# A hybrid decoder layer on one core: side work tied to its stage, down products in column pairs, the last product closed half by half

## The chip, the cores and the metric

The kernel runs on one core of a Trainium2 chip. The metric is the device time of one execution in microseconds. Before the change three runs gave 2251.72 us as the median, from 2249.6 to 2251.99 us. A core has TensorE (PE, with its weight loads shown as PEld), VectorE (DVE), ScalarE (ACT), GpSimd (POOL) and SyncE (SP), which here issues nearly all transfers. Each engine works through its own list of instructions in order; what one needs from another it waits for.

## The reference

One layer over 2048 tokens of width 1024, all in float32:

```
mod = silu(c) @ w_ada + b_ada                     # six rows of 1024: shift, scale, gate, twice
h = rmsnorm(x) * (1 + scale1) + shift1
q, k, v, z, xbc, dt = split(h @ w_in)             # 2312 columns
attn = sliding_window_attention(rope(q), rope(k), v, sinks)      # window 128
y = gated_norm(ssd_chunked_scan(silu(conv(xbc)), dt), z)
x = x + gate1 * (concat(attn, y) @ w_out)
h = rmsnorm(x) * (1 + scale2) + shift2
x = x + gate2 * ((silu(h @ w_gate) * (h @ w_up)) @ w_down)       # width 2816
return rmsnorm(x) * final_w
```

## The kernel before, in words

The tokens are worked in four blocks of 512. Every float32 product is made of three products of rounded parts: each operand is split into a high part (written by ACT) and a low part (raw minus high, by DVE), and PE adds high*high, high*low and low*high into one PSUM bank (`mm3`, L274). So every weight and every activation costs an ACT and a DVE instruction before PE can use it.

The stages in order: an opening with the norm of block 0 and its modulation; the input projections of blocks 0 to 3 (`queries`, `keys_values`, `convolved`, `gated`), beside which attention and the SSD scan of earlier blocks are stepped ("sides"), and the output projections of blocks 0 and 1; then gate and up products of the first half of the tokens (`quads(0, ...)`), the output projections of blocks 2 and 3 (`first_output`, `second_output`), three down stages of the first half (`down0.stage`), gate and up of the second half (`quads(1, ...)`), and eleven more down stages. Gate/up and down use Strassen-like products: seven products of halves each, named b11, b21, t4, t2, t3, t1, b22; the down ones need sums of `w_down` blocks, made by `weight_sums` (L1048) and stored to `wd_s1` to `wd_s4`.

A loop that runs over main work calls `tick` after each step; a tick counts down `pending` entries, takes one step of the remaining modulation rows (`rest_of_ada`) and steps the sides by a ratio. This gives the order in which the code is traced. PE keeps it up to the end of the input projections (`manual_schedule`); DVE, ACT, POOL and SP are ordered by a scheduler that places an instruction as soon as its own estimate says that it can run, so an instruction without early inputs can stand far ahead of the code that traced it. `tc.issue_after(i)` keeps what is traced inside it behind instruction `i`.

Names to follow: `aw` are halves of `w_ada` rows (L192 loads, L197 reduces them on DVE with the row `csil`); `t` is a ring of eight 128x512 buffers (`tmp`); `hl` are the split activations of a block; `a` are split activations of the down stages; `ws` the blocks in `weight_sums`; `d`, `am`, `at`, `sm`, `st` are PSUM banks (four `d`, one of each other). `mid` is the residual in DRAM. In `steps_of` (L1075) a down stage has four output columns c, each with eleven k in three chunks, one weight tile per chunk.

Of the kernel before, what the change touches and what calls it, by code (L numbers as in the profile page):

```python
# [12 lines left out]
F32 = mybir.dt.float32  # L13
# [5 lines left out]
P = 128  # L19
# [25 lines left out]
def hymba_layer(ctx, tc, xT, xtok, pos, wada, wadk, vecs, rows, wq, wkv, wz, wx, wo, wgu, wd, outT):  # L45
# [140 lines left out]

    def ada_later(i):
        halves = [slice(0, T), slice(T, D)]
        ws = [big("aw", 2, pool=ip) for _ in halves]
        with tc.issue_after(mm3.last.ins):  # L190
            for w, hs in zip(ws, halves):
                nc.sync.dma_start(w, wada[i, :, hs])  # L192
# [3 lines left out]
        for w, hs, src, dst in zip(ws, halves, (b_ada[:, i:i + 1], pt), (pt, m)):  # L196
            nc.vector.tensor_tensor_reduce(w, w, csil[:, hs], 0.5, src, ALU.mult, ALU.add, dst)  # L197
# [126 lines left out]
    def modulated(x, bc, scale, shift, into):  # L324
        h = tmp()
        nc.vector.scalar_tensor_tensor(h, x, scale, bc, ALU.mult, ALU.mult)
        hi, lo = into
        nc.scalar.activation(hi, h, AF.Identity, bias=shift)
        modulated.last = nc.vector.scalar_tensor_tensor(lo, h, shift, hi.bitcast(F32), ALU.add, ALU.subtract)  # L329
        return hi, lo  # L330
# [16 lines left out]
    def norm1(b, h):  # L347
# [13 lines left out]
        yield  # L361
        for d in range(KT):
            h.append(modulated(load_x(b, d), bc, scl1[:, d:d + 1], sh1[:, d:d + 1], operand()))
        yield
# [190 lines left out]
    def attentions(b, m):  # L555
# [26 lines left out]
        held, nxt = None, load(0)  # L582
        for t in range(NT):
# [281 lines left out]
    def scaled(s, k, bc, which):  # L865

        h = {}
        for i, j in which:
            d = k + 4 * i
            x = h[i, j] = tmp()  # L870
            scaled.last = nc.sync.dma_start(x, mid[2 * s + j][d])
# [16 lines left out]
    def operands_first(s, ops, bc):  # L888

        for k in range(4):  # L890
            h = scaled(s, k, bc, ((0, 0), (1, 0)))
# [156 lines left out]
    def weight_sums(pool):  # L1048

        n = KP * P // 4  # L1050
        for c in range(4):
            for q in range(4):
                cs = slice(q * n, (q + 1) * n)
                a11, a21, a22, a12 = (small([P, n], "ws", 4, pool=pool) for _ in range(4))
                for x, (i, h) in ((a11, (0, 0)), (a21, (1, 0)), (a22, (1, 1)), (a12, (0, 1))):
                    nc.sync.dma_start(x, wd[c + 4 * i, h][:, cs])
                nc.vector.tensor_tensor(a11, a11, a21, ALU.subtract)
                nc.vector.tensor_tensor(a21, a21, a22, ALU.add)
                nc.vector.tensor_tensor(a22, a22, a11, ALU.subtract)
                nc.vector.tensor_tensor(a12, a12, a22, ALU.subtract)  # L1060
# [14 lines left out]
    def steps_of(act, src, banks, new, done, ts=slice(0, T), kept_w=None):  # L1075

        for c in range(4):
            if new:
                banks[c] = dense()
            ps = banks[c][:, ts]  # L1080
            for lo, hi in CHUNKS:
                key = c, lo
                if kept_w is not None and key in kept_w:
                    w = kept_w[key]
                else:
                    n = (hi - lo) * P
                    raw = wt.tile([P, 528], F32, name="raw", tag="raw", bufs=RAW)[:, 0:n]
                    nc.sync.dma_start(raw, src(c)[:, lo * P:hi * P])
                    if kept_w is None:
                        two = wt.tile([P, 2, 528], F32R, name="w", tag="w", bufs=SPLIT)  # L1090
                        w = two[:, 0, 0:n], two[:, 1, 0:n]
                    else:
                        a, b = pair("a", KP + 1, pool=steps_of.spare)
                        w = kept_w[key] = a[:, 0:n], b[:, 0:n]
                    nc.scalar.activation(w[0], raw, AF.Copy)  # L1095
                    nc.vector.tensor_tensor(w[1], raw, w[0].bitcast(F32), ALU.subtract)  # L1096
                for k in range(lo, hi):
                    ws = slice((k - lo) * P, (k - lo + 1) * P)
# [3 lines left out]
                if hi == KP:  # L1102
                    done(c, ps)
# [574 lines left out]
```

## Time and profile before

| what | value |
|---|---|
| median of three runs | 2251.72 us |
| the profiled execution's own time | 2250.91 us |
| its span | 2249.2 us |
| PE busy | 2172.1 us, 97% of the span |
| DVE busy | 1676.9 us, 75% |
| ACT, POOL busy | 1009.8 us, 573.6 us |
| transfers | 469.93 MB, mean 209 GB/s |

The profiled execution's time is 1.7 us above its span, and 0.8 us below the median. PE is the engine to read: what it does not work, or works at the lower clock, is the time that can be had; DVE is what it mostly waits for.

### The profile page before, as it was taken

The numbers are of one execution on the slowest core, as the hardware profiler recorded it, in microseconds if no ns is written. First come the engines' busy times: TensorE is split into PE (matmuls) and PEld (weight loads), VectorE is DVE, ScalarE is ACT, GpSimd is POOL, SyncE is SP. The second block draws the span as 40 slices with busy tenths as digits, with TensorE's granted clock in tenths as the row PEclk, the third lists the DMA queues.
The fourth block names the chain that finished last, engine by engine and source line by source line (L and its number), as shares of the span: only waits on it lengthen the run. The fifth ranks groups of instructions, "written<-read, shape, count | busy, mean of one in ns | idle before, by whom it ended". The sixth has DMA issues, their size and how long they took to land. (4 is left out here: it accounts for less than half of the span.)

```text
span 2249.2 us, 33574 instructions
## 1 busy us (share of the span) xinstructions
PE 2172.1 (97%) x11108; PEld 1806.9 (80%) x11108; DVE 1676.9 (75%) x3219; ACT 1009.8 (45%) x2135; POOL 573.6 (26%) x715
## 2 busy tenths in 40 slices
PE   8988999899999999999999999998999999999997
PEld 6877898789878788888888877786888888788887
DVE  8988876676569877788887667988767775786565
ACT  4564634554545654433344444532333333554342
POOL 0122433233112311144442311222323331220021
PEclk9999999999999999999999999999999999999999
DMA  8999988785879522333435678967323326777553
GB/s 288 333 396 310 325 264 302 235 285 186 294 267 309 168 85 93 101 119 106 127 103 164 222 251 281 348 210 233 116 94 113 99 90 206 260 265 266 173 171 101
DMA packets 289181, 469.93 MB, mean 209 GB/s; under 512 B 27376, under 2 KB 97008, under 8 KB 289008
## 3 DMA queue, kind: packets, MB, share of 16 engines
q1 hardware_dynamic: 288432, 467.27, 62.4%
q8 instruction: 87, 1.43, 0.3%
q14 instruction: 86, 0.70, 0.1%
q10 hardware_dynamic: 576, 0.52, 0.1%
HBM read 334.98 MB, written 132.71 MB: 208 GB/s over the span
## 5 line engine op out<-in xcount | busy, mean ns | idle before, releaser
L1100 PE MATMUL d<-a,w 128*128 128x512 f32 x1716 | 404.7, 396 | 5.6 <-DVE a L1072 2.6
L1100 PEld LDWEIGHTS d<-a,w 128*128 128x128 f32 x1716 | 321.5, 188 | 85.8 <-DVE a L1072 4.5
L961 PE MATMUL d<-b,w 128*128 128x512 f32 x924 | 367.8, 401 | 4.3 <-ACT t L985 3.4
L962 PE MATMUL d<-b,w 128*128 128x512 f32 x924 | 367.1, 397 | 3.0 <-DVE b L883 2.2
L963 PE MATMUL d<-b,w 128*128 128x512 f32 x924 | 366.6, 398 | 1.9 <-DVE w L853 1.9
L852 ACT ACTIVATE w<-s 128x512 fp32r<-128x512 f32 x176 | 110.7, 631 | 231.1 <-PE d L963 177.5
L961 PEld LDWEIGHTS d<-b,w 128*128 128x128 f32 x924 | 174.3, 189 | 45.0 <-ACT t L985 4.3
L962 PEld LDWEIGHTS d<-b,w 128*128 128x128 f32 x924 | 175.0, 189 | 42.8 <-DVE b L883 2.9
L963 PEld LDWEIGHTS d<-b,w 128*128 128x128 f32 x924 | 174.3, 189 | 42.0 <-DVE w L853 2.4
L275 PE MATMUL d<-w,hl 128*128 128x256 f32 (+1 forms) x592 | 174.7, 295 | 11.3 <-DVE so L504 3.1
L277 PE MATMUL d<-w,hl 128*128 128x256 f32 (+1 forms) x592 | 169.9, 287 | 3.2 <-DVE hl L329 2.9
L276 PE MATMUL d<-w,hl 128*128 128x256 f32 (+1 forms) x592 | 169.7, 287 | 0.8 <-DVE w L1310 0.8
L1096 DVE TENSOR_TENSOR w<-raw,w 128x512 fp32r<-128x512 f32 x156 | 105.8, 685 | 60.0 <-ACT w L1095 59.7
L853 DVE TENSOR_TENSOR w<-s,w 128x512 fp32r<-128x512 f32 x176 | 141.6, 806 | 9.7 <-ACT w L852 8.6
L285 POOL TENSOR_TENSOR acc<-acc,t 128x512 f32<-128x512 f32 x35 | 60.0, 1715 | 347.5 <-ACT t L284 338.3
L1095 ACT ACTIVATE w<-raw 128x512 fp32r<-128x512 f32 x156 | 91.1, 589 | 121.2 <-PE d L1100 83.5
L275 PE MATMUL d<-hl,w 128*128 128x512 f32 x352 | 144.8, 411 | 0.4 <-DVE s L385 0.4
L277 PE MATMUL d<-hl,w 128*128 128x512 f32 x352 | 139.3, 396 | 0.0
L276 PE MATMUL d<-hl,w 128*128 128x512 f32 x352 | 138.9, 395 | 0.2 <-DVE hl L812 0.2
L852 ACT ACTIVATE w<-raw 128x512 fp32r<-128x512 f32 x132 | 82.8, 630 | 115.2 <-PE d L963 45.6
L1072 DVE TENSOR_TENSOR a<-a 128x512 fp32r<-128x512 f32 x154 | 103.0, 694 | 36.8 <-ACT a L1071 36.5
L275 PEld LDWEIGHTS d<-w,hl 128*128 128x128 f32 x592 | 114.6, 194 | 15.5 <-DVE so L504 3.8
(420 smaller groups left out, 4919.7 us busy)
## 6 DMA issues: line engine op xcount, KB each, us to landing
raw<-in_wgu_dram SPq DMA_DIRECT2D x176, 256.0 KB, 2.8
w<-w_x SPq DMA_DIRECT2D x48, 512.0 KB, 5.3
act_t<-t SPq DMA_DIRECT2D x88, 256.0 KB, 3.2
a<-act_t SPq DMA_DIRECT2D x88, 256.0 KB, 4.7
act_b<-t SPq DMA_DIRECT2D x66, 256.0 KB, 2.1
a<-act_b SPq DMA_DIRECT2D x66, 256.0 KB, 4.8
aw<-in_wada_dram SPq DMA_DIRECT2D x64, 256.0 KB, 4.8
raw<-wd_s SPq DMA_DIRECT2D x64, 256.0 KB, 2.7
```

The costliest lines, as they stand in the source:

```text
L275: nc.tensor.matmul(out, ahi, bhi, start=first, stop=False)
L276: nc.tensor.matmul(out, ahi, blo, start=False, stop=False)
L277: mm3.last = nc.tensor.matmul(out, alo, bhi, start=False, stop=last)
L852: nc.scalar.activation(hi, x, AF.Copy)
L853: eng.tensor_tensor(lo, x, hi.bitcast(F32), ALU.subtract)
L961: nc.tensor.matmul(out, ahi, bhi, start=first and k == 0, stop=False, skip_group_check=True)
L962: nc.tensor.matmul(out, ahi, blo, start=False, stop=False, skip_group_check=True)
L963: mm3.last = nc.tensor.matmul(out, alo, bhi, start=False, stop=k == 3, skip_group_check=True)
L1072: nc.vector.tensor_tensor(lo, raw, hi.bitcast(F32), ALU.subtract)
L1095: nc.scalar.activation(w[0], raw, AF.Copy)
L1096: nc.vector.tensor_tensor(w[1], raw, w[0].bitcast(F32), ALU.subtract)
L1100: mm3.last = nc.tensor.matmul(ps, w[x][:, ws], act[k][y][:, ts], start=new and k == 0 and x + y == 0, stop=k == KP - 1 and x == 1, skip_gr ...
```

## The change: what it does

It has eight parts, with the lines of the new kernel in the order below.

1. **Modulation rows.** A helper `behind(engine)` gives an `issue_after` on the last instruction traced on that engine. The `aw` loads stand behind the last traced SP instruction, the reduces behind the last traced DVE instruction.
2. **Norm.** `modulated` works in place instead of through a second `t` buffer; `norm1` takes a block's eight columns in two halves, each half's loads one step ahead of its work. The tick numbers in `norm_ahead` change to match.
3. **Attention.** `attentions` yields once after its first load, and that step is taken at tick 10 of `convolved(0)`.
4. **Second norm's operands.** `operands_first` loads `mid` for step k+1 before it works on step k, and its DVE products stand behind the last traced DVE instruction.
5. **Output projection of block 3** uses the four `d` banks in place of `am` and `at` in turn.
6. **Weight sums.** Loads behind SP, sums behind DVE, with a step between them; 32 steps in place of 16, at twice the rate in `quads(1, ...)`.
7. **Down stages.** `steps_of` goes over columns in pairs: chunk 0 of both, chunk 1 of both, chunk 2 of both. The ratio of the side work beside the first three stages is 0.3 in place of 0.5, and the next stage's first eight `a` tiles are asked for at steps 8 and 9.
8. **Last product.** Still two halves of 256 tokens, but PE's order is now the code's, the squares' sums of half 0 are added on PE inside the next column, and half 0's root, spread and eight outputs are stepped inside half 1.

```diff
+    def behind(engine):
+        traced = nc.cur_bb.bb.instructions
+        return tc.issue_after(next(i for i in reversed(traced) if i.engine == engine))
...
-        with tc.issue_after(mm3.last.ins):
+        with behind(mybir.EngineType.SP):
             for w, hs in zip(ws, halves):
                 nc.sync.dma_start(w, wada[i, :, hs])
...
+        with behind(mybir.EngineType.DVE):
+            for w, hs, src, dst in zip(ws, halves, (b_ada[:, i:i + 1], pt), (pt, m)):
+                nc.vector.tensor_tensor_reduce(w, w, csil[:, hs], 0.5, src, ALU.mult, ALU.add, dst)
...
+        for ds in (range(KT // 2), range(KT // 2, KT)):
+            xs = [load_x(b, d) for d in ds]
+            yield
+            for d, x in zip(ds, xs):
+                h.append(modulated(x, bc, scl1[:, d:d + 1], sh1[:, d:d + 1], operand()))
+            yield
...
         held, nxt = None, load(0)
+        yield
...
+        x = fetched_mid(s, 0, which)
+        yield
         for k in range(4):
-            h = scaled(s, k, bc, ((0, 0), (1, 0)))
+            nxt = fetched_mid(s, k + 1, which) if k < 3 else None
+            with behind(mybir.EngineType.DVE):
+                h = scaled(s, k, bc, which, x)
+            x = nxt
...
+                with behind(mybir.EngineType.SP):
+                    for x, (i, h) in ((a11, (0, 0)), (a21, (1, 0)), (a22, (1, 1)), (a12, (0, 1))):
+                        nc.sync.dma_start(x, wd[c + 4 * i, h][:, cs])
+                yield
+                with behind(mybir.EngineType.DVE):
+                    nc.vector.tensor_tensor(a11, a11, a21, ALU.subtract)
...
-        for c in range(4):
-            if new:
+        for c, (lo, hi) in ((c + e, chunk) for c in (0, 2) for chunk in CHUNKS for e in range(2)):
+            if new and lo == 0:
                 banks[c] = dense()
...
+                        if at == 1:
+                            while late:
+                                late.pop(0)()
+                        step = part * (3 * c + at)
+                        for _ in range((step == 2 or step > 3) + (step == 6)):
+                            next(ends[0], None)
+                        yield
+                    done(part, c, ps)
...
-        yield from output(3)
+        yield from output(3, lambda c: dense())
...
-            if i >= 14 and i % 7 == 0:
+            if i >= 14 and i % 7 in (0, 4):
                 next(sums_of, None)
...
-        with tc.manual_schedule(engines={mybir.EngineType.DVE}) if is_last else nullcontext():
+        with tc.manual_schedule(engines={mybir.EngineType.DVE, mybir.EngineType.PE}) if is_last else nullcontext():
```

On DVE in the opening stood, before, reduces of late modulation rows (L197) between the splits of block 0's first weights and activations (L1310 to L1312):

```order
L1311 SCALAR_TENSOR_TENSOR hl_557<-t,mod,hl_557 128x512
L1310 TENSOR_TENSOR w<-raw,w 128x512
L197 ISA aw,part<-aw,csil,vec 128x512
L197 ISA part 128x1
L1311 SCALAR_TENSOR_TENSOR hl_561<-t,mod,hl_561 128x512
L1312 TENSOR_TENSOR w<-raw,w 128x528
L1304 SCALAR_TENSOR_TENSOR t<-m_267,scl_145,at 128x512
```

After the change the same place holds the opening's own work (L1323 are the opening's modulation rows, L1344 to L1352 the scaling and splits):

```order
L1323 ISA m_394,mod<-m_394,csil,vec 128x1024
L1323 ISA mod 128x1
L1326 SCALAR_TENSOR_TENSOR scl_145<-mod,vec 128x1
L184 SCALAR_TENSOR_TENSOR mod<-am,vec 128x2 x2
L185 SCALAR_TENSOR_TENSOR scl_145<-mod,vec 128x2
L1344 SCALAR_TENSOR_TENSOR t<-m_263,scl_145,at 128x512
L1344 SCALAR_TENSOR_TENSOR t<-m_265,scl_145,at 128x512
L1350 TENSOR_TENSOR w<-raw,w 128x512
```

The 64 reduces now stand, two and two, among the rows of blocks 1 to 3.

On DVE around the end of the third down stage and the start of the second half's gate/up stood, before, the sums of `w_down` blocks (L1057 to L1060), between splits of weights (L853), of `a` (L1072) and the stage's last reads of PSUM (L1131):

```order
L853 TENSOR_TENSOR w<-s,w 128x512 x2
L1057 TENSOR_TENSOR ws<-ws 128x352
L853 TENSOR_TENSOR w<-s,w 128x512
L1072 TENSOR_TENSOR a<-a 128x512
L1131 SCALAR_TENSOR_TENSOR t<-d,mod,t 128x512
L971 TENSOR_TENSOR s<-raw 128x512
L853 TENSOR_TENSOR w<-s,w 128x512
L1058 TENSOR_TENSOR ws<-ws 128x352
```

After it they stand in the middle of that gate/up, among its own rows (L860 splits, L1007 to L1056 the product's sums):

```order
L860 TENSOR_TENSOR w<-raw,w 128x512
L1052 TENSOR_TENSOR t<-t 128x512
L1007 SCALAR_TENSOR_TENSOR t<-t,d 128x512
L1077 TENSOR_TENSOR ws<-ws 128x352
L860 TENSOR_TENSOR w<-raw,w 128x512
L1028 TENSOR_TENSOR t<-t,d 128x512
L1078 TENSOR_TENSOR ws<-ws 128x352
L860 TENSOR_TENSOR w<-s,w 128x512
L1079 TENSOR_TENSOR ws<-ws 128x352
```

The first sum moved from beside the down stages to some way into the gate/up that follows them.

On PE at the program's end, before, half 0's last sum of squares (L1212 into `am`) stood 7 products ahead of the end of the last product (L1100, 264 instructions of 256 columns), and its spread (L321 into `st`) behind the end:

```order
L1100 MATMUL d<-a 128x256 x162
L1212 MATMUL am<-ones,sqs 128x2 x2
L1100 MATMUL d<-a 128x256 x30
L1212 MATMUL am<-ones,s 128x2 x2
L1100 MATMUL d<-a 128x256 x65
L1212 MATMUL am<-ones,s 128x2 x2
L1100 MATMUL d<-a 128x256 x7
L321 MATMUL st<-t,ones 128x256
```

After it (L1251 the product, L1223 the sums, L326 the spread):

```order
L1251 MATMUL d<-a 128x256 x123
L1223 MATMUL am<-ones,sqs 128x2 x2
L1223 MATMUL am<-ones,s 128x2 x2
L1251 MATMUL d<-a 128x256 x33
L1223 MATMUL am<-ones,s 128x2 x2
L1251 MATMUL d<-a 128x256 x33
L326 MATMUL st<-t,ones 128x256
L1251 MATMUL d<-a 128x256 x66
L1223 MATMUL at<-ones,sqs 128x2 x2
```

Half 0's last sum moved to 108 products ahead of the end, and its spread to 75.

## Rows read from the trace of the kernel before

**Rows 1.** The page's first part: busy time, share of the span, instructions of each engine.

```profile
PE 2172.1 (97%) x11108; PEld 1806.9 (80%) x11108; DVE 1676.9 (75%) x3219; ACT 1009.8 (45%) x2135; POOL 573.6 (26%) x715
```

**Rows 2.** Stretches of the span: from:to, length, busy us (instructions) of PE, PEld, DVE, ACT, POOL, then the mean granted clock (1.00 is 2.4 GHz), the share of the transfer engines, GB/s.

```profile
25.00:325.00 300.00, 276.28 (x1802) 242.63 (x1803) 254.11 (x655) 151.70 (x352) 73.98 (x119) 0.97 0.92 321
325.00:640.00 315.00, 307.41 (x1943) 269.75 (x1942) 199.18 (x546) 163.25 (x434) 88.53 (x187) 0.99 0.79 260
640.00:760.00 120.00, 112.38 (x661) 93.97 (x660) 107.80 (x206) 71.78 (x159) 34.33 (x33) 1.00 0.80 266
1300.00:1325.00 25.00, 20.54 (x78) 15.71 (x77) 16.15 (x36) 8.92 (x14) 2.63 (x2) 0.86 0.67 229
1375.00:1425.00 50.00, 46.27 (x193) 35.46 (x192) 49.04 (x76) 32.06 (x58) 13.82 (x7) 1.00 0.97 335
1500.00:1550.00 50.00, 43.23 (x172) 33.80 (x171) 41.48 (x63) 12.38 (x23) 11.81 (x8) 0.93 0.77 247
1550.00:1875.00 325.00, 325.00 (x1404) 263.62 (x1404) 234.93 (x309) 108.28 (x183) 101.47 (x67) 1.00 0.36 112
1875.00:2200.00 325.00, 323.11 (x1400) 260.68 (x1399) 211.30 (x362) 152.24 (x269) 40.79 (x23) 1.00 0.68 227
```

**Rows 3.** What PE waited for between 25 and 325 us: engine, tile and line that waits, what released it, us in total, times, longest.

```profile
PE at L594 <- DMA m<-q: 4.7, 1, 4.7
PE at L321 <- DVE t L319: 3.3, 1, 3.3
PE d L275 <- DVE so L504: 3.1, 2, 2.7
PE d L277 <- DVE hl L329: 2.9, 3, 1.4
PE d L275 <- ACT hl L328: 2.8, 1, 2.8
PE d L275 <- DVE s L492: 2.7, 1, 2.7
```

**Rows 4.** The same of the rest: 325 to 640 us, 640 to 760, 1300 to 1425, 1475 to 1550 and 1920 to 1940, the largest of each.

```profile
PE st L719 <- ACT m L798: 3.5, 1, 3.5
...
PE d L962 <- DVE b L883: 2.2, 2, 1.4
...
PE am L275 <- DVE t L828: 3.7, 1, 3.7
PE d L1100 <- DVE a L1072: 2.6, 4, 1.6
...
PE d L961 <- ACT t L985: 3.4, 1, 3.4
...
PE d L1100 <- DVE w L1096: 1.9, 2, 1.0
```

**Rows 5.** The reduces' line: duration in ns min/median/max, first and last start, shape; what DVE waited for there (us, times); and in the last row what else DVE waited for between 640 and 760 us.

```profile
L197 DVE CUSTOM_DVE_ANT_0 aw<-aw,csil,vec x32: 723/746/949, 37.5 to 317.1; 128x512 f32<-128x512 f32 x32
L197 DVE CUSTOM_DVE_ANT_0 aw<-aw,csil,part x32: 716/746/1192, 40.7 to 321.0; 128x512 f32<-128x512 f32 x32
  DMA aw<-in_wada_dram: 17.9, 12
...
DVE t L872 <- DMA t<-mid: 3.9, 4, 2.7
```

**Rows 6.** Pieces of the chain that ended last: start us, length us, what.

```profile
1504.14 3.82 DMA ws<-in_wd_dram
...
1509.63 3.04 DMA wd_s<-ws
1512.73 2.66 DMA ws<-in_wd_dram
...
1542.22 0.43 PE d L961
...
2042.53 143.96 PE d L1100 x621
```

**Rows 7.** DVE in order of time at 1308 us: start us, us, instruction, idle before it and what ended that.

```profile
1308.81 0.75 DVE L872 SCALAR_TENSOR_TENSOR t<-t,scl,bc 128x512 f32<-128x512 f32 x1 [1.25 <-DMA t<-mid]
...
1310.90 0.75 DVE L828 SCALAR_TENSOR_TENSOR t<-am,mod,t 128x512 f32<-128x512 f32 x1
```

**Rows 8.** The end: PE, ACT and DVE in order of time from 2233 us.

```profile
2233.84 1.07 PE L1100 MATMUL d<-a 128*128 128x256 f32 x7
...
2241.67 1.19 PE L321 MATMUL sm<-t,ones 128*128 128x256 f32 x2 [1.92 <-DVE t L319]
...
2236.75 0.42 ACT L1206 ACTIVATE s<-x 128x256 f32<-128x256 f32 x1 [2.34 <-DVE x L1204]
...
2235.70 0.41 DVE L1203 TENSOR_TENSOR u<-u,d 128x256 f32<-128x256 f32 x1
2236.15 0.48 DVE L1204 SCALAR_TENSOR_TENSOR x<-u,mod,x 128x256 f32<-128x256 f32 x1
...
2239.84 0.14 DVE L307 TENSOR_SCALAR qr<-at 128x2 f32<-128x2 f32 x1
...
2241.04 0.48 DVE L319 TENSOR_SCALAR t<-ident,qr 128x128 f32<-128x128 f32 x2
...
2243.01 3.22 DVE L1235 SCALAR_TENSOR_TENSOR t<-x,vec,sm 128x256 f32<-128x256 f32 x8
```

More of the change, by code (lines that the diff above doesn't have):

```diff
@@ L1073, in tokens_of, with steps_of @@
             yield hi, lo
-    def steps_of(act, src, banks, new, done, ts=slice(0, T), kept_w=None):
-        for c in range(4):
-            if new:
+    def steps_of(act, src, banks, new, done):
+        for c, (lo, hi) in ((c + e, chunk) for c in (0, 2) for chunk in CHUNKS for e in range(2)):
+            if new and lo == 0:
                 banks[c] = dense()
[L1080 to L1098, printed above, removed]
-                    for x, y in ((0, 0), (0, 1), (1, 0)):
-                        mm3.last = nc.tensor.matmul(ps, w[x][:, ws], act[k][y][:, ts], start=new and k == 0 and x + y == 0,
-                                                    stop=k == KP - 1 and x == 1, skip_group_check=True)
-                if hi == KP:
-                    done(c, ps)
-                yield
@@ new lines, in steps_of @@
+            ps, n = banks[c], (hi - lo) * P
+            raw = wt.tile([P, 528], F32, name="raw", tag="raw", bufs=RAW)[:, 0:n]
+            nc.sync.dma_start(raw, src(c)[:, lo * P:hi * P])
+            two = wt.tile([P, 2, 528], F32R, name="w", tag="w", bufs=SPLIT)
+            w = two[:, 0, 0:n], two[:, 1, 0:n]
+            nc.scalar.activation(w[0], raw, AF.Copy)
+            nc.vector.tensor_tensor(w[1], raw, w[0].bitcast(F32), ALU.subtract)
+            for k in range(lo, hi):
+                ws = slice((k - lo) * P, (k - lo + 1) * P)
+                for x, y in ((0, 0), (0, 1), (1, 0)):
+                    mm3.last = nc.tensor.matmul(ps, w[x][:, ws], act[k][y], start=new and k == 0 and x + y == 0,
+                                                stop=k == KP - 1 and x == 1, skip_group_check=True)
@@ L1222, in last @@
+            while late:
+                late.pop(0)()
             drain(ends[0])
@@ L1580, in hymba_layer @@
             nxt, coming = ring(0, after, dn, KP) if after else (None, None)
-            for i in beside(down0.stage(name, act), 0.5):
-                if after and i >= 8:
-                    for _ in range(4 if i < 10 else 3):
+            for i in beside(down0.stage(name, act), 0.3):
+                if after and i in (8, 9):
+                    for _ in range(4):
                         next(coming, None)
```

129 lines of the change are left out of this document (73 added, 56 removed).

## The prediction

> **What bounds the kernel now.** The page's busy times come first: PE works 97% of the span, DVE 75% [rows 1]. So no engine but PE can set the whole, and what can be had is PE's idle time and the time in which PE works at the lower of its two clocks. The table of stretches says where that is [rows 2]: from 1550 to 1875 us, in the second half's gate and up, PE is busy 325.00 of 325 us at a granted clock of 1.00 (2.4 GHz), and nothing is to be won; from 25 to 325 us it idles 23.7 us at a mean clock of 0.97, from 1500 to 1550 us 6.8 us at 0.93, from 1300 to 1325 us 4.5 us at 0.86. The lists of PE's waits name the releasers [rows 3, 4]: nearly all are DVE instructions or splits that DVE and ACT make, and one is a transfer (q). What DVE itself waits for is the next view: 17.9 us for `aw` in twelve waits, all in the stretch where PE loses most [rows 5], and for `ws` and `mid` further on [rows 5 to 7]. DVE takes its instructions in order, so an early one that waits for a transfer holds the ones that PE needs.
>
> **What the lower clock costs.** In a stretch after a stop one product of 512 columns takes 0.43 us (1.2 GHz), in steady work 143.96 / 621 = 0.232 us [rows 6]. So a microsecond at the lower clock loses 1 - 0.232 / 0.43 = 0.46 us. A mean clock c over L us means 2 (1 - c) L us at the lower one.
>
> **The terms, each against the profiled execution's 2250.91 us** (2249.2 of span and 1.7 around it, 0.8 below the median).
>
> *Block 0 and 1's projections, 25 to 325 us.* Idle 23.7 us, of which 3.3 wait for the opening's spread (L319), ahead of all that moves: 20.4 can go. Clock 0.97: 18 us at the lower one, 8.3 us lost. Together 28.7. The change takes out 64 reduces of 0.746 us, 47.7 us [rows 5], and their 17.9 us of waits, so DVE is left with 206 of 300 us, 69%. The next stretch, 325 to 640 us, is the same kind of work with DVE at 63%: it idles 7.6 us of 315 at clock 0.99 (6.3 us, 2.9 lost) [rows 2], 10.5 in all, or 10.0 per 300 us. I let the first stretch become like it: 28.7 - 10.0 = **-18.6**. It is at least the waits that hang on late loads and modulation alone, q 4.7 and `hl` 2.9 + 2.8 [rows 3], -10.4; at most -28.7. The norm's split and attention's early load are in this term: the in-place product costs what it cost, and the loads only stand earlier.
>
> *325 to 640 us.* By the order of DVE some 27 of 32 modulation rows land here: 54 x 0.746 = 40 us, DVE from 199 to 239 of 315, 76%. Between 63% with 10.5 us lost and 85% with 28.7 per 300 (30.1 per 315) a straight line gives 22, or +11.6. But a good part of the loss at 85% was DVE held by `aw`, and a reduce now has two steps between load and use. I take half, **+6**; from -4 (some of the 7.6 us of idle time goes with earlier norm loads) to +18.6 (all that the first stretch gains comes back here).
>
> *640 to 760 us.* DVE is busy 107.8 of 120 us, so work added shows: five rows, ten reduces, +7.5. The loads of `mid` one step ahead take away DVE's 3.9 us of waits [rows 5], which stand before PE's waits for `b` (2.2) [rows 4]. 7.5 - 3.9 = **+3**, rounded down since not all of it is before a wait of PE; from -3.9 to +7.5.
>
> *1300 to 1325 us, output projection of block 3.* PE stops 3.7 us for L828, DVE's read of a bank two columns back [rows 4]; DVE was at L872, waiting for `mid` [rows 7]. Idle 4.5, clock 0.86 (7 us, 3.2 lost): 7.7. Four banks instead of two and the earlier loads take both causes. **-6.5**, the spread's short wait stays; from 0 (if DVE is late for another reason) to -7.7.
>
> *1375 to 1425 us, between the first down stages.* PE idles 3.7 us, for `a` (2.6 by L1072 alone) [rows 2, 4], with DVE busy 49.04 of 50. The next stage's `a` need the buffers of this one. In pairs the first four are free after step 7, the next four after step 9, against 9 and 10 of 12 before, a new stage needs its fifth only after 24 products instead of 12, and the side work and `ws` beside it thin out. **-3**, from 0 to -3.7. The 1.9 us at the second half's end (L1096) [rows 4] have the same cure: **-1.5**, from 0 to -1.9.
>
> *1500 to 1550 us.* The chain of waits runs through `ws`: a load of 3.82 us, a store of 3.04, the next load of 2.66, since four buffers serve one round [rows 6]; DVE sits before them, and PE waits for its splits, 3.4 us in one piece [rows 4]. Idle 6.8, clock 0.93 (7 us, 3.2 lost): 10.0. Each load now has three or four steps of the gate/up before its sums. The sums go to 1550 to 1875 us, where DVE has 90 us free. **-9**, from -3 (waits of DVE stay, in a place with slack) to -10.
>
> *The end.* From the last product (2234.9) to the end of the span are 14.3 us [rows 8]. Half 0 leaves this tail. What stays in line is 0.41 + 0.48 for the residual, 0.42 for its square, 1.68 from L307 to the end of L319, 1.19 for the spread, 3.22 for eight outputs and 2.97 behind the last output: 10.4, with about 1.4 of hand-overs (an estimate from the 0.12 to 0.3 us between those rows, and the sum on PE) 11.8. **-2.5**; from 0 to -3.9.
>
> *Other down stages.* The last two columns now end together, so two reads of banks come at once; the next stage starts on banks freed half a stage before, which hides it. Without that cover 13 stages cost a read of 0.75 us each [rows 7], 9.8. **+2**, from 0 to +9.8.
>
> Sum: -18.6 + 6 + 3 - 6.5 - 3 - 1.5 - 9 - 2.5 + 2 = -30.1; 2250.9 - 30.1 + 0.8 = **2221.5 us** against the median.
>
> A rule speaks against the pairs. In the second half's gate/up PE goes to another bank after every twelve products and yet is busy throughout at clock 1.00 [rows 2]. The Trainium skill (TensorE: Matmul & The Clock Gate, "A second HAM failure mode: psum-queue depth-cycling") says that cycling through PSUM banks can leave small idle gaps between groups, so that the clock falls and rises again; the trace disagrees here, so it has a small chance below.
>
> **The rivals.**
>
> *The waits move with the reduces.* The loss per microsecond of DVE's work does not fall, and the middle gives back what the start gains. For it: DVE at 76% and the transfer engines at 0.79 before 54 loads of 128x512 words, 14 MB, more [rows 2]. Against it: twelve of the waits were DVE's own, for loads that stood without any step between. +18.6 in place of +6: 2234.
>
> *Slower: the `aw` loads hold SP.* Two buffers serve a row, so the next row's loads wait in SP's list until DVE has reduced the last, and every weight load behind them waits too. If each of 32 rows costs PE what an `aw` wait cost DVE, 17.9 / 12 = 1.5 us, that is +48 in place of +6, and the time is 2221.5 + 42 = 2263. It decides from 36 us of such waits on, 1.1 us per row. For it: the weights of blocks 2 and 3 come through the same queue. Against it: a row has three steps, and DVE's backlog is short where DVE is at 76%. The Trainium skill (DMA: Bandwidth & Descriptors, "Anatomy of one DMA — SWDGE (gpsimd) path") says that a transfer's wait for a semaphore is made on the issuing sequencer before dispatch, which is this mechanism; no row here prices it.
>
> *Bank pairs lose the clock.* Thirteen stages with one fall like that at 1300 us, 3.2 us each, +42: 2263 too.
>
> *The parts do nothing together.* The start gains its least (-10.4), the middle returns it, the down stages lose 9.8 against the 19.5 that the later places give, and two of these keep their waits: 2249.
>
> *All goes.* First stretch -25, middle 0, the rest at its ends: 2207.
>
> **How the numbers follow.** Forecast 0.55 (its own range 2211 to 2232), waits moved 0.20, all goes 0.12, nothing together 0.05, SP held 0.06, bank pairs 0.02. A measurement of this kernel tells 0.2% (4.5 us) from no change. Faster: 0.55 + 0.20 + 0.12 = 0.87; the same 0.05; slower 0.08. The range takes in the moved waits with a few us and stops short of the best and the two slow cases: 2205 to 2243.
>
> **What would show it.** Right: no reduces before 325 us in the new trace, PE idle there under 12 us, no wait of PE for q or `hl` over 2 us; PE idle under 2 us in the stretches that answer to 1300 and 1500 us, both at clock 1.00; sums of `ws` spread over the whole second gate/up; the last product's end 11 to 12 us before the end. Wrong: PE idle between 325 and 760 us over 30 us, waits named `aw`, or `raw` and `w` loads that come late there; a clock under 1.00 in the down stages, which now have 1.00 and PE busy 323.11 of 325 us [rows 2]; a tail of 14 us.

## The result and the profile after

The changed kernel takes **2232.84 us** (median of four runs, 2229.64 to 2235.22) against 2251.85 us for the kernel before beside it: a ratio of **0.9915 [0.9898, 0.9932]**, or 19.0 us less. The forecast was 2221.5 us, 30 us less; the range of 2205 to 2243 us holds the time, and it falls almost on the price of the rival in which the waits move with the reduces (2234). The forecast itself was 11.3 us too low. The profiled execution after is the longest of the four, 2235.22 us with a span of 2233.2 us.

The page's busy times answer to [rows 1]:

```profile
PE 2167.6 (97%) x11108; PEld 1808.3 (81%) x11108; DVE 1692.5 (76%) x3219; ACT 1011.3 (45%) x2137; POOL 572.5 (26%) x715
```

PE executes the same 11108 products, with 11.0 us less of stops inside (59.7 us by the gaps between products, 70.7 before). The table of stretches answers to [rows 2], with the same columns. The place that was at 1300 us lies some ten us earlier now, so its stretch is taken wider:

```profile
25.00:325.00 300.00, 284.96 (x1916) 254.20 (x1917) 230.03 (x590) 159.43 (x372) 83.14 (x137) 0.98 0.83 281
325.00:640.00 315.00, 297.09 (x1813) 255.69 (x1812) 221.25 (x607) 157.99 (x415) 82.23 (x168) 0.97 0.85 289
640.00:760.00 120.00, 108.18 (x604) 90.67 (x603) 103.06 (x213) 66.22 (x152) 32.17 (x32) 0.93 0.84 280
1275.00:1350.00 75.00, 75.00 (x327) 60.60 (x327) 55.66 (x85) 32.12 (x56) 17.16 (x12) 1.00 0.77 259
1375.00:1425.00 50.00, 49.32 (x214) 39.72 (x213) 48.24 (x72) 32.32 (x60) 13.63 (x7) 1.00 0.91 315
1500.00:1550.00 50.00, 50.00 (x217) 40.55 (x216) 41.64 (x56) 16.69 (x28) 16.13 (x11) 1.00 0.57 176
1550.00:1875.00 325.00, 325.00 (x1404) 263.65 (x1403) 255.10 (x347) 108.60 (x184) 96.00 (x64) 1.00 0.49 157
1875.00:2200.00 325.00, 322.65 (x1448) 262.73 (x1448) 229.75 (x375) 153.69 (x271) 40.52 (x27) 1.00 0.70 232
```

Two halves of a story stand there. From 1275 us on PE no longer stops and the clock is 1.00 in each of the places that the change aimed at. Before 760 us the first stretch won (PE idles 15.0 us in place of 23.7), but the next lost as plainly: idle 17.9 us of 315 in place of 7.6, the clock at 0.97, and 0.93 from 640 us.

Adding the times at which the n-th product of the program ends says it in microseconds. Each column is a place, named by its time in the kernel before; each number is the profiled execution of a kernel minus that of before, counted from the first product's end (the row of the changed kernel: 14.0 us ahead at 317 us, 13.7 us late at 767 us).

```
                                317   767  1138  1269  1346  1421  1491  1571  2197
changed kernel                -14.0  13.7   9.2   8.5   0.7  -3.6  -2.7 -13.2 -13.0
rows alone                    -20.2  -0.2  -4.8  -4.0  -4.5  -5.3  -5.2  -5.0  -4.8
rows undone                     2.2  18.8  14.3  13.9   6.1   1.1   1.9  -8.6  -7.7
short reduces                 -14.9   6.3   1.7   1.0  -6.8 -12.5 -11.0 -21.5 -21.3
no row loads                  -12.5  13.8   9.6   8.9   1.1  -4.5  -3.9 -14.4 -14.2
norm undone                   -19.7   2.1  -2.7  -3.4 -11.2 -16.9 -16.1 -26.6 -26.5
attention undone               -9.9   7.5   8.5   9.3   1.6  -2.5  -1.7 -12.2 -12.2
norm, attention undone        -18.9   0.8   1.7   2.6  -5.1  -9.1  -7.8 -18.3 -18.3
these and operands undone     -20.2   6.1   1.5   2.1  -5.7  -9.9  -8.3 -18.7 -18.6
norm and rows undone            3.7  20.8  16.0  15.3   7.5   2.5   3.3  -7.2  -7.0
norm's split alone              2.9  10.6   8.9   9.2   9.1   8.6   8.8   9.5   9.0
eight rows moved later        -17.4   5.1 117.3 121.9 114.1 108.4 109.0  98.6  99.6
last product and pairs alone    0.6   6.1   4.2   4.2   4.6  -1.1  -1.2  -2.1  -0.8
```

Up to 767 us such a number is good to some 6 us only: the row at the bottom has PE's work in the order of before up to the down stages, and is 6.1 us late there. Single runs of one kernel spread by 4 to 14 us, so the verdicts below go by the ratios. (One of the twelve runs of the kernel with the rows alone took 6060.69 us, for no cause that the record shows; its ratio leaves that run out.) From 1138 us on the steps agree within about a microsecond wherever the same edits are in. (From 1009 to 1138 us the kernel before idles 2.3 us, with the clock at 0.99; some of the kernels do so and some don't, whatever their edits, so the 4.9 us that the changed kernel gains there are put down to none.)

What PE waits for from 25 to 325 us, and from 325 to 760 us, answers to [rows 3, 4]; columns as there:

```profile
PE d L280 <- DVE s L498: 4.8, 1, 4.8
PE at L326 <- DVE t L324: 3.3, 1, 3.3
PE at L640 <- DVE m L605: 2.2, 1, 2.2
PE am L640 <- ACT m L604: 1.7, 1, 1.7
PE at L601 <- DMA m<-q: 1.6, 1, 1.6
...
PE am L281 <- DVE m L678: 7.5, 6, 3.2
PE st L726 <- ACT m L805: 4.5, 1, 4.5
PE st L326 <- DVE t L324: 3.4, 1, 3.4
```

The waits for q and `hl` that the forecast took away are gone or under 1.7 us. The wait for the convolution's read of a bank in block 0 (L498, L492 before) has grown from 2.7 us [rows 3] to 4.8, and in the middle PE waits for attention's probabilities (`am` for L678) 7.5 us in place of 3.6. Before the change this was already the largest wait from 640 to 760 us, ahead of the one for `b` that [rows 4] gives as the largest:

```profile
PE am L276 <- DVE m L671: 2.4, 3, 1.5
```

The end answers to [rows 8]:

```profile
2220.72 1.31 PE L1251 MATMUL d<-a 128*128 128x256 f32 x9
2222.07 0.42 DVE L1229 TENSOR_TENSOR u<-u,d 128x256 f32<-128x256 f32 x1 [2.73 <-PE d L1251]
...
2226.06 1.19 PE L326 MATMUL sm<-t,ones 128*128 128x256 f32 x2 [1.88 <-DVE t L324]
2227.29 3.22 DVE L1275 SCALAR_TENSOR_TENSOR t<-x,vec,sm 128x256 f32<-128x256 f32 x8 [1.38 <-PE sm L326]
```

From the last product (2222.0) to the end of the span are 11.2 us, 3.1 less than before. Half 0's outputs are out of that tail.

### The profile page after: what moved, and what is told of

Its sections match the earlier page's. It is cut to its first block, busy times and chain, and to the rows that moved or that the text cites. A ratio compares the mean times of both kernels' runs of the same rounds, so it can differ in the third digit from the quotient of the medians.

```text
span 2233.2 us, 33604 instructions
## 1 busy us (share of the span) xinstructions
PE 2167.6 (97%) x11108; PEld 1808.3 (81%) x11108; DVE 1692.5 (76%) x3219; ACT 1011.3 (45%) x2137; POOL 572.5 (26%) x715
## 4 chain that ended last, share of the span: by engine, by line
PE 83%; DVE 7%; DMA 6%; issue 2%; ACT 2%; POOL 1%; SPq 0%; DVEq 0%; ACTq 0%; POOLq 0%
PE d L1110 16%; PE d L980 9%; PE d L978 9%; PE d L979 9%; PE d L280 5%; PE d L281 5%; PE d L282 5%; PE d L1251 1%; PE am L980 1%; PE am L978 1%; PE am L979 1%; DMA t<-in_xT_dram 1%; PE sm L791 1%; PE am L281 1%; PE am L282 1%
## 5 line engine op out<-in xcount | busy, mean ns | idle before, releaser
L860 DVE TENSOR_TENSOR w<-s,w 128x512 fp32r<-128x512 f32 x176 | 155.4, 885 | 5.0 <-ACT w L859 4.7
L280 PE MATMUL d<-hl,w 128*128 128x512 f32 x352 | 146.9, 417 | 1.3 <-DMA w<-w_x 1.3
L1092 DVE TENSOR_TENSOR a<-a 128x512 fp32r<-128x512 f32 x154 | 108.5, 716 | 49.7 <-ACT a L1091 49.3
L290 POOL TENSOR_TENSOR acc<-acc,t 128x512 f32<-128x512 f32 x35 | 50.9, 1454 | 360.8 <-ACT t L289 322.6
L1106 DVE TENSOR_TENSOR w<-raw,w 128x512 fp32r<-128x512 f32 x156 | 113.3, 736 | 39.4 <-ACT w L1105 39.3
L281 PE MATMUL d<-hl,w 128*128 128x512 f32 x352 | 140.6, 399 | 1.0 <-DVE hl L819 1.0
L282 PE MATMUL d<-hl,w 128*128 128x512 f32 x352 | 140.7, 400 | 0.0
L1091 ACT ACTIVATE a<-a 128x512 fp32r<-128x512 f32 x154 | 96.1, 628 | 85.0 <-DMA a<-act_t 51.0
```

The source lines that it names most:

```text
L280: nc.tensor.matmul(out, ahi, bhi, start=first, stop=False)
L281: nc.tensor.matmul(out, ahi, blo, start=False, stop=False)
L282: mm3.last = nc.tensor.matmul(out, alo, bhi, start=False, stop=last)
L860: eng.tensor_tensor(lo, x, hi.bitcast(F32), ALU.subtract)
L1091: nc.scalar.activation(hi, raw, AF.Copy)
L1092: nc.vector.tensor_tensor(lo, raw, hi.bitcast(F32), ALU.subtract)
```

## The experiments

### The rows alone

The kernel before, with the loads and reduces of the modulation rows tied and nothing else:

```diff
-        with tc.issue_after(mm3.last.ins):
+        with behind(mybir.EngineType.SP):
             for w, hs in zip(ws, halves):
                 nc.sync.dma_start(w, wada[i, :, hs])
...
+        with behind(mybir.EngineType.DVE):
+            for w, hs, src, dst in zip(ws, halves, (b_ada[:, i:i + 1], pt), (pt, m)):
```

> The kernel before with one part of the change alone: the loads of a modulation row stand behind SP's last traced instruction and its two reduces behind DVE's. Theory A (the waits move with the reduces: what the first stretch gains, the middle gives back): by the stretches of the changed kernel the first gives 14 us and the stretch from 325 to 767 us takes up to 27.7, so the time is 5 to 14 us above the kernel before (2257 to 2266), PE idles under 14 us from 25 to 325 us, and the product that ends at 767 us comes at least 8 us late. Theory B (the rows are a gain, and the middle is lost to the other edits there: norm loads in halves, attention's first load early, operands fetched a step ahead): 8 to 14 us below the kernel before (2238 to 2244). Theory C (part 1 does nothing for the time by itself): within 3 us of it.

Measured: 2251.04 us, ratio 0.9986 [0.9971, 1.0], 3.2 us less. The stretches show what lies beneath:

```profile
25.00:325.00 300.00, 291.01 (x1969) 258.70 (x1970) 227.45 (x577) 157.19 (x371) 84.54 (x142) 0.99 0.85 289
325.00:640.00 315.00, 297.97 (x1814) 255.44 (x1812) 226.39 (x605) 159.62 (x417) 79.53 (x164) 0.99 0.87 293
```

In the start PE idles 9.0 us in place of 23.7, and the products are 20.2 us ahead at 317 us, more than the forecast's 18.6. At 767 us they are 0.2 us ahead: the middle returned 20.0 us. Six of the 64 reduces start before 325 us, 50 from there to 640 us, eight later. By the time it is nearest to theory C; by the stretches it is theory A's give and take, though the product at 767 us does not come 8 us late. What follows: with the rows alone the loss moves, and little of the gain is kept.

### The rows undone

The changed kernel with these lines as before:

```diff
-        with behind(mybir.EngineType.SP):
+        with tc.issue_after(mm3.last.ins):
...
-        with behind(mybir.EngineType.DVE):
```

> The changed kernel with that part undone: row loads stand behind the last product traced, the reduces go where the order puts them, as before. Theory A: the stretch from 325 to 767 us is 20 us or more shorter than in the changed kernel, the first one about 14 longer, so 2220 to 2228 against 2232.8. Theory B: the loss in the middle stays, and the first stretch's 14 us are gone: 2244 to 2250. Theory C: 2230 to 2236. The forecast's own terms (-18.6 for the first stretch, +6 and +3 for the middle) would give about 2242.

2241.58 us, 0.9949 [0.9931, 0.9966]: 8 us above the changed kernel by the ratios, and what the forecast's own terms had said (2242), outside of all three theories' ranges. But the middle is no better for it. The table has 2.2 at 317 us and 18.8 at 767 us: with the reduces back in the start, the other early edits lose 16.6 us after it by themselves. So tied rows are not the only thing that costs the middle, and the two losses don't add.

### What of a row costs: short reduces, and no loads

Two kernels take one half of a row's cost away and keep the order of the code (the scheduler then places some of DVE's and ACT's instructions otherwise). In the first a reduce has 8 columns; in the second the loads are out, and the reduce reads the sums' vector.

```diff
-                nc.vector.tensor_tensor_reduce(w, w, csil[:, hs], 0.5, src, ALU.mult, ALU.add, dst)
+                nc.vector.tensor_tensor_reduce(w[:, 0:8], w[:, 0:8], csil[:, 0:8], 0.5, src, ALU.mult, ALU.add, dst)
```

```diff
-                nc.sync.dma_start(w, wada[i, :, hs])
...
-                nc.vector.tensor_tensor_reduce(w, w, csil[:, hs], 0.5, src, ALU.mult, ALU.add, dst)
+                nc.vector.tensor_tensor_reduce(w, csil[:, hs], csil[:, hs], 0.0005, src, ALU.mult, ALU.add, dst)
```

> The changed kernel with the 64 later reduces cut to 8 of their 512 columns, all loads of rows kept. Most of the sums of the modulation rows are left out, so their result is not the reference's. This takes some 64 x 0.65 = 42 us of work from DVE, 35 of it between 325 and 767 us, and leaves the transfers and DVE's waits for them. If DVE's work is what the middle pays for (0.5 us of PE's time for 1 us of DVE's, which the straight line of the forecast had about twice too low): 12 to 22 us less, 2211 to 2221. If DVE's waits for the rows' loads or the transfers themselves are what counts: at most 5 us less, 2228 or more, and more such waits than the 15.2 us of the changed kernel.

> The changed kernel without the 64 later loads of rows of w_ada; the reduces keep their size and place and read the vector of sums that is on the chip already. The loads are left out, so the modulation of the later rows is not the reference's. This takes 64 transfers of 128x512 words (16.8 MB) and DVE's 15.2 us of waits for them, and leaves DVE's work. If the waits or the transfers are what the middle pays for: 12 to 22 us less than 2232.8, 2211 to 2221, with the waits for row loads gone. If it is DVE's work: at most 5 us less, 2228 or more. If both count alike, this run and the one with short reduces each take 6 to 12 us.

2227.16 us, 0.9887 [0.9864, 0.991], and 2229.89 us, 0.9893 [0.9871, 0.9915]: 6.3 and 5.0 us less than the changed kernel, each within the uncertainty of the two ratios. The stretch from 325 to 775 us, with the short reduces and then without loads:

```profile
325.00:775.00 450.00, 423.06 (x2519) 362.99 (x2518) 315.01 (x844) 233.66 (x581) 116.66 (x203) 0.97 0.83 282
...
325.00:775.00 450.00, 419.90 (x2503) 358.62 (x2503) 338.83 (x837) 230.39 (x578) 116.93 (x204) 0.97 0.74 246
```

With short reduces DVE is busy 315 us there, less than the 320.7 of the kernel before, and PE still idles 27 us (15 before, 30 in the changed kernel). So DVE's busy share is not the price, as the forecast's straight line had it. A short reduce still takes 0.22 us, so DVE lost 29.5 us of work in the whole program and not the 42 expected, and the time 6.3 us where 12 to 22 were expected; by the uncertainty of the two ratios this work may be part of the price, but not all of it. Nor are the transfers: without the loads their share is 0.74 in place of 0.83, and PE idles 30.1 us in place of 29.7. Both keep the reduces tied. That the order itself (a reduce tied behind DVE's last instruction, with attention's steps queued behind it) holds attention up was only argued. Another rival stands untested: that something else sets when the projections end, so that no lead from the start can be kept. No execution in the table has its product at 767 us more than 0.2 us ahead of the kernel before, though six are 14.9 to 20.2 us ahead at 317 us.

The slower rival, rows that hold SP's queue, falls here: it asked for 1.5 us a row, 48 us in all, and the kernel without the loads gains 5 us. In the changed kernel SP does wait at these loads for the reduces, 14.9 us in fifteen waits from 270 to 710 us; the larger of its two rows:

```profile
SPq L196 <- DVE part L202: 10.8, 8, 5.8
```

With the rule of the Trainium skill that was named beside the rival (DMA: Bandwidth & Descriptors, "Anatomy of one DMA — SWDGE (gpsimd) path"), that the issuing sequencer makes the wait for a semaphore, this agrees; the price is no more than those 5 us.

### The norm's split undone, attention's first load undone, both, and the operands too

Four kernels take early edits back from the changed kernel: the norm's split; attention's first load; both; and with both the first half's operands. One line of each edit stands for it:

```diff
-        for ds in (range(KT // 2), range(KT // 2, KT)):
-            xs = [load_x(b, d) for d in ds]
-            yield
-            for d, x in zip(ds, xs):
-                h.append(modulated(x, bc, scl1[:, d:d + 1], sh1[:, d:d + 1], operand()))
-            yield
+        yield
+        for d in range(KT):
+            h.append(modulated(load_x(b, d), bc, scl1[:, d:d + 1], sh1[:, d:d + 1], operand()))
+        yield
...
-        pending.append([10, lambda: next(att)])
...
-            nxt = fetched_mid(s, k + 1, which) if k < 3 else None
+            nxt = fetched_mid(s, k + 1, which) if s and k < 3 else None
```

> The changed kernel with the norm's split undone (x loaded and modulated in one step of eight, into a tile of its own, at the steps of before). The rows alone gave back in the middle all that they won in the start, and the changed kernel without the rows still lost 18.8 us up to 767 us. Theory D (the norm's split costs it): the product that ends at 767 us comes at the time of the kernel before or earlier (-3 to +4 in place of +13.7), ratio 0.985 to 0.988. Theory E (attention's early first load costs it): it stays at +10 to +14, ratio 0.990 to 0.993. Theory F (the operands of the feed-forward fetched a step ahead, with DVE's place fixed, cost it): as theory E, up to 600 us unchanged from the changed kernel.

> The changed kernel with attention's early first load undone. Theory E: the gap of attention's first steps near 157 us goes, the product at 767 us comes at -3 to +4, ratio 0.985 to 0.988. Theories D and F: +10 to +14 stays, ratio 0.990 to 0.993.

> Both undone, the rest of the change kept. Theories D and E: up to 767 us the products run as in the kernel with the rows alone, -20 at 316 us and 0 at 767 us, and the 29 us that the later parts give remain: ratio 0.986 to 0.988 to the kernel before, about 14 us under the changed kernel. Theory F: the loss of 8 to 14 us comes between 600 and 767 us, ratio 0.990 to 0.993.

> As the last, and the first half's operands fetched as before (the second half's still a step ahead). Theories D and E: within 3 us of the last run. Theory F: 8 to 14 us less than it, the gain between 600 and 767 us.

2225.47 us, 0.9889 [0.9865, 0.9913]; 2233.81 us, 0.9919 [0.9897, 0.9941]; 2229.99 us, 0.9903 [0.9884, 0.9922]; 2223.81 us, 0.988 [0.9857, 0.9902]. Attention's first load is worth nothing that these can tell, and theory E falls. Without the norm's split the products are at +2.1 us in place of +13.7 at 767 us, theory D's number, though by the ratios only 6 us of it are there, which is within their uncertainty (the profiled execution was the shortest of its four). With both undone the ratio is 0.9903, where theory D had 0.986 to 0.988. With the first half's operands undone as well, the time is 5 us less, where theory F had 8 to 14 and D had 3 at most, and 0.35% below the changed kernel: the two intervals overlap only from 0.9898 to 0.9902. So none of the three theories has all of its numbers.

For the start the table is clearer. At 317 us the four kernels with the rows tied and the norm's split are 9.9 to 14.9 us ahead, the five with the rows tied and without it 17.4 to 20.2. Where the rows are not tied, the split changes little there (2.2 with it, 3.7 without).

The trace says how a load that comes earlier can go with a cost. The line of the norm's products on DVE, first in the changed kernel, then with the split undone (columns: shortest/median/longest ns, first and last start):

```profile
L330 DVE SCALAR_TENSOR_TENSOR t<-t,scl,bc x8: 737/740/1306, 113.3 to 129.1; 128x512 f32<-128x512 f32 x8
...
L331 DVE SCALAR_TENSOR_TENSOR t<-t,scl,bc x8: 739/744/753, 122.3 to 170.6; 128x512 f32<-128x512 f32 x8
```

With the split undone the eight products stand over 48 us in DVE's order, with the convolution's work between them. DVE idled for a load before only two of them, 3.2 us in all, so it is their places in the order, more than the waits, that spread them. With the loads early the eight stand within 16 us: six start between 113.3 and 117.9 us with second parts (L333) among and behind them, and the last two (127.86 and 129.12) stand just ahead of the convolution's read of its bank (L498), for which PE waits (DVE's row, then PE's; start us, us, instruction, idle before it):

```profile
130.45 0.74 DVE L498 SCALAR_TENSOR_TENSOR s<-d,vec,s 128x512 f32<-128x512 f32 x1
...
131.24 0.58 PE L280 MATMUL d<-w,hl 128*128 128x256 f32 x1 [4.81 <-DVE s L498]
```

That is the wait of 4.8 us. With the rows alone, and with the split undone, it is not among PE's waits.

### The norm's split and the rows undone; the split alone

The changed kernel with the rows' lines and the norm's both undone, and the kernel before with that of the norm alone, of which these lines stand for the rest:

```diff
-        for d in range(KT):
-            h.append(modulated(load_x(b, d), bc, scl1[:, d:d + 1], sh1[:, d:d + 1], operand()))
+        for ds in (range(KT // 2), range(KT // 2, KT)):
+            xs = [load_x(b, d) for d in ds]
+            yield
```

> The changed kernel with the norm's split and the tied rows both undone. If the rows only move the loss (-20 in the start, +20 in the middle), this comes within 4 us of the run with the norm's split undone (2225.5): at 316 us its products run at -3 to +3 against the kernel before, at 767 us too, and the later parts give some 29 us: ratio 0.986 to 0.990. If the rows are worth the 7.6 us that undoing them cost the changed kernel: 2230 to 2236, ratio 0.990 to 0.9925.

> The kernel before with the norm's split alone (x loaded a step ahead, in halves, modulated in place, at the steps of the changed kernel). If the split is what the middle lost: 8 to 16 us over the kernel before, all of it up to 767 us, with several of the norm's products in one row on DVE near 115 us and PE waiting there for the convolution's read of a bank; ratio 1.0035 to 1.007. If it only costs where the rows are tied too: within 4 us of the kernel before.

2240.57 us, 0.9945 [0.9925, 0.9964], and 2253.7 us, 1.0008 [0.9996, 1.0019]. The first is above both of its expectations, the second where the split was to cost only beside tied rows. The first says that the rows are worth 12.6 us once the split is out (0.9945 to 0.9889), the second that the split alone costs 1.8 us, not resolved from nothing; its profiled execution was the longest of ten, so 10.6 in the table says too much. Yet the wait for the convolution's read (here L493) is in it, on the wait list of PE from 110 to 175 us, larger than the 2.7 us of before:

```profile
PE d L275 <- DVE s L493: 6.5, 3, 3.3
```

The first run's 20.8 us at 767 us come with neither the rows nor the split. What is left of early edits there is attention's first load with its extra step, and the operands' fetch. The later edits' gain, 24.6 us in the changed kernel (21.5 from 1269 to 2197 us in the table, 3.1 in the tail), should give 0.989, so some 12 us are lost to these two, and as much with the split in (the run with the rows undone). Neither was taken back alone there, so which of the two it is was not shown. When the rows are tied, the same two cost 2 us, not resolved from nothing (0.9889 against 0.988). Why they cost more with the reduces in the start stays open; PE waits there for q (3.9 us) and `hl` (4.0 and 3.0) as it did before.

### The last product and the pairs alone

The kernel before with the new steps of the down stages and the new close (`last` and `final` as changed):

```diff
-        for c in range(4):
-            if new:
+        for c, (lo, hi) in ((c + e, chunk) for c in (0, 2) for chunk in CHUNKS for e in range(2)):
+            if new and lo == 0:
```

> The kernel before with the down stages in column pairs and the last product's closing alone. The forecast has -3 between the first two down stages, +2 (0 to +9.8) for the other stages, -1.5 at the second half's wait and -2.5 at the end: 4 to 6 us less than the kernel before, all of it after 1340 us, ratio 0.997 to 0.9985, the clock 1.00 in the down stages. If the pairs cost a read of a bank in every stage: 2 to 6 us more than before. If the changed kernel's gain at 1346 to 1421 us (4.3 us) comes from the earlier loads and not from the pairs: under 2 us there.

2243.17 us, 0.9956 [0.9942, 0.997], 9.9 us less (6.8 to 13.1) where 4 to 6 were expected. In the trace 5.7 us go between 1346 and 1421 us, 1.3 come back in the later stages, and some 3 go in the tail; the rest of the 9.9 is not found there. Its stretch from 1350 to 1425 us:

```profile
1350.00:1425.00 75.00, 75.00 (x326) 60.32 (x325) 63.24 (x112) 38.20 (x68) 15.09 (x8) 1.00 0.90 314
```

PE never stops there, at clock 1.00; in the kernel before it idled 3.7 us. Part 7 does that (the pairs, the thinner side work and the earlier `a` together; they were not taken apart), and not the earlier loads of the other parts. So the pairs lose no clock: from 1875 to 2200 us the changed kernel has a granted clock of 1.00 with PE busy 322.65 of 325 us. The trace still disagrees here with what the Trainium skill (TensorE: Matmul & The Clock Gate, "A second HAM failure mode: psum-queue depth-cycling") reports of another kernel that cycled through banks.

### Eight rows moved to where PE never idles

From 775 to 1030 us PE is busy throughout and DVE 200 of 255 us. The norm's split undone, the last eight rows were put there, each half row through two of the eight `t` tiles:

```diff
+                w, cs = tmp(), tmp()
+                with behind(mybir.EngineType.SP):
+                    nc.sync.dma_start(w, wada[i, :, half * T:(half + 1) * T])
+                    nc.sync.dma_start(cs, csil_d[half])
+                yield
+                with behind(mybir.EngineType.DVE):
+                    nc.vector.tensor_tensor_reduce(w, w, cs, 0.5, src, ALU.mult, ALU.add, dst)
```

> The changed kernel with the norm's split undone, and the last eight of the 32 rows (the second gate's, first read in the down stages) moved to the first half's gate and up, 780 to 1020 us, where PE never idles and DVE has slack; there the vector of sums comes from memory beside each half row. If a reduce costs time only where PE waits for DVE: the middle gives back 20 to 22 us for 27 rows, so 8 rows less are 4 to 7 us less, no loss after 780 us, and the time is 2218 to 2222, ratio 0.984 to 0.987. If the place of the rows does not matter: within 3 us of 2225.5.

2349.1 us, 1.042 [1.0399, 1.0441]: 124 us more than the 2225.47 without the move, and outside of both expectations. The stretch in question, with the move and without:

```profile
775.00:1030.00 255.00, 187.48 (x787) 146.21 (x787) 142.67 (x298) 90.19 (x245) 73.23 (x107) 0.71 0.27 84
...
775.00:1030.00 255.00, 255.00 (x1269) 209.00 (x1268) 199.54 (x366) 120.12 (x282) 63.72 (x65) 1.00 0.34 107
```

PE idles 67.5 us and runs over half the stretch at the lower clock. The groups of PE's work from 775 to 900 us tell why, again with the move and without:

```profile
L280 PE MATMUL am<-m,v_ring 128*128 128x256 f32 x32 | 13.1, 409 | 16.0 <-ACT m L667 12.2 <-ACT m L676 2.4 <-DVE m L677 1.4
L977 PE MATMUL d<-b,w 128*128 128x512 f32 x9 | 3.7, 409 | 0.0
...
L977 PE MATMUL d<-b,w 128*128 128x512 f32 x149 | 59.0, 399 | 0.0
```

The gate's products, 149 on this line, had filled attention's waits. With the move nine are left beside it, for PE's order now holds attention's steps nearly alone, and the gate's products follow later. Sixteen reduces of some 0.8 us do not make 124 us, and DVE is busy less than without the move; the changed order of PE does. What pushed the gate's products back (the `t` tiles held over a step, or the loads in SP's list) was not tried.

## Why the prediction was right, and where it was not

**The later places** were forecast at -6.5 (1300 us), -3 (1375 us), -9 (`ws`), -1.5, +2 (other stages) and -2.5 (the end), -20.5 together. In the table they give -7.8 (1269 to 1346), -4.3 (1346 to 1421), -10.5 (1491 to 1571), +0.2 (1571 to 2197), and -3.1 at the tail. All kernels with these edits show the first within 0.1 us of 7.8 and the third at 10.4 or 10.5, those without them at under 1 us either way. These two were read as idle time plus what the clock loses beside it, 7.7 and 10.0 before the forecast took something off, and the whole of it went. Each of the four that gained came out 0.6 to 1.5 us better than forecast. Which of its two causes (two banks, or the load of `mid`) made the stop at 1300 us was not taken apart.

**The first stretch** was forecast at -18.6; the rows alone gave -20.2. The changed kernel has -14.0, since a sentence of that step failed: "the in-place product costs what it cost, and the loads only stand earlier". With the loads earlier the norm's products come in a row, ahead of the convolution's read, and the kernels with the split have less of a lead there than those without it.

**The middle** is the step that failed: "I take half, +6" from 325 to 640 us, and +3 to 760 us, +9 against +27.7 measured (good to some 6 us). The two sums before they were halved or reduced, +11.6 and +7.5, give 19.1, and the rows alone cost 20.0; every kernel with the rows tied loses 17.4 to 27.7 us between 317 and 767 us in the table. The reason for the halving (a reduce has two steps between its load and its use) did not hold: the waits moved with the reduces. DVE in the changed kernel, from 325 to 775 us:

```profile
DVE aw L202 <- DMA aw<-in_wada_dram: 13.6, 10, 3.8
DVE t L835 <- DMA t<-in_xT_dram: 5.5, 3, 2.1
```

Ten waits of 13.6 us stand against twelve of 17.9 us in the start [rows 5]. But the sum was right by a wrong working: the runs with short reduces and without loads show that neither DVE's busy share nor these waits is what PE pays for one by one. What it pays for stays open. And the other early edits, priced at nothing in the middle, lose there too: 16.6 and 17.1 us in the two kernels that have them, or most of them, without the tied rows. What the rows are worth depends on them: 3.2 us alone, 7.7 with all the rest, 12.6 without the split. Set against the later edits' 24.6 us, no ratio on record leaves more than some 3 us of gain to the early edits, and that of the changed kernel leaves a loss of 5.5.

So the forecast named the places and the sizes of the later half, and one rival had the early half's outcome. That the time came so near this rival's 2234 is in part luck: its start was 4.6 us too good and its middle 6.1 us too small, and the later places' extra 4 us and the 5.2 us between 767 and 1269 us, put down to no edit, made up for it. Signs that were asked for: no reduces before 325 us (six of 64, missed); PE idle from 25 to 325 us under 12 us (15.0, missed; 9.0 with the rows alone); no wait for q or `hl` over 2 us (met); no stops and clock 1.00 at 1300 and 1500 us (met); sums of `ws` over the whole second gate/up (nearly: from 1494.9 to 1793.6 us, of 1445 to 1876); last product 11 to 12 us before the end (11.2, met); PE idle between 325 and 760 us over 30 us as a sign of error (29.7, on the edge), and so were waits named `aw` there (13.6 us, which came); a clock under 1.00 in the down stages and a tail of 14 us did not come.

The experiments point to a version that is better than both kernels, though its interval still touches the changed kernel's: the rows tied, the norm's split, attention's load and the first half's operands as before, and all later edits. It took 2223.81 us, 0.988 of the kernel before; with the norm's split alone undone it was 2225.47 us, not told apart from it.

## What to carry to other kernels

Moving work out of a stretch that waits need not gain: here the next stretch had the same kind of waits, and returned 20.0 of 20.2 us. Nor is slack on the engine that gets the work enough, since sixteen reduces cost 124 us where DVE had 55 us free. Price such a move at the same rate in both places, without a discount, and look for places where the stops are local (a bank, four buffers, a stage's border), since there the forecast held within 1.5 us. A load fetched earlier can also change where the scheduler puts the work that reads it; ask what will then run in one piece, and who stands behind.

## What was not expected of the hardware

Two sizes surprised. Taking 16.8 MB of loads out of the changed kernel (the share of the transfer engines from 325 to 775 us fell from 0.83 to 0.74) left PE's idle time there as it was, 29.7 and 30.1 us. And a stretch that had PE busy for 255 of 255 us at 2.4 GHz fell to a mean granted clock of 0.71 when attention's products lost the gate's products between them: with 67.5 us of idle time and the low clock it was 117.3 us behind the kernel before at 1138 us (2.7 ahead without the move), more than all that this change won.
